# A mixture-of-experts block with one weight tile in an eleventh place, and its residual set up one expert later

## The chip, the cores and the metric

The kernel runs on one core of one Trainium2 chip. The metric is the device time of one execution in microseconds (us); the time quoted is the median over the runs of a kernel. Where a profile is read, it is one execution recorded by the hardware profiler, whose times count from the start of its span. TensorE is PE in the rows (PEld is its weight load), VectorE is DVE, ScalarE is ACT, GpSimd is POOL, and SyncE is SP; SP issues the transfers of the weights.

## What is computed

Two transformer blocks on 256 tokens of width 1024, all in fp32. The first is attention with 8 heads, a layer norm, a mixture of 32 experts with the best 4 for each token, and a layer norm. The second is a mixer of a gated linear recurrence and a short convolution, and a convolutional feed-forward network. The change lies in the mixture of experts, cut here to what matters:

```python
logits = xt @ w_router + b_router
top_logit, top_e = lax.top_k(logits, 4)
gate = softmax(top_logit)
# for each expert e, on the tokens that chose it:
h = xb @ w_gu[e] + b_gu[e]                    # [1024] -> [2048]
h_gate, h_up = split(h)
h_gate = minimum(h_gate, 7); h_up = clip(h_up, -7, 7)
act = h_gate * sigmoid(1.702 * h_gate) * (h_up + 1)
f = act @ w_down[e] + b_down[e]               # [1024] -> [1024]
# y = ALPHA * layer_norm(...) + sum over a token's experts of gate * f
```

Each expert has 8 MB of gate and up weights and 4 MB of down weights, so the 32 experts read 384 MB.

## The kernel before, in words

The experts go in order, 0 to 31, in batches of two, with 64 rows for each expert. For a batch the rows of its tokens are gathered by products with a one-hot matrix (`pgat`, L694) and the gates are put in place (`pw`, L763). For one expert `gate_up` (L777 to L800) multiplies four tiles of gate and up weights, c = 0 to 3, of 2 MB each, into the banks `pg` and `pu`. `swiglu` (L769 to L775) turns them into `at`, with four operations on VectorE and one on ScalarE. `transpose_act` transposes `at` by four products (`atp`, L805). `down_half` multiplies two tiles of down weights into `pd` (L818). Down products of expert e are issued one turn of the loop later, behind the gate and up products of expert e + 1, and with the last one of a batch the result is added into y, a tile named `xtok`.

y must hold its start value before that: `start_y` (L658 to L680) broadcasts the rows of the layer norm's gain and bias by eight small products into banks `lnr` (L259), scales and shifts the normed tokens on VectorE (L666 and L668, eight operations of 512 columns), transposes the gates (`gp`, L672), copies them (`GT`, L673), multiplies them with the down biases `bdn` (`pb`, L678, four products, eight instructions in the trace) and adds these to y (L679, four operations). In the kernel before it is called in the turn of expert 0.

The weights stream through ten places of 2 MB: six in a pool whose tiles are named `w` and four in one whose tiles are named `wb`. A list `loads` holds all transfers in order: first the attention's, then for each expert four gate and up tiles and the two down tiles of the expert before. In this text the 192 transfers of the experts are numbered from 1. `pump` (L183) issues the next ones on SP's queue, and `weight` asks it for nine tiles ahead of the one that is about to be multiplied. The n-th transfer takes the place of the (n - 10)-th, so SP waits until TensorE has multiplied that tile. SP's queue is in order: a transfer that waits holds all behind it.

Which instruction stands where on an engine is set by a scheduler that works on the program as it is written, except where `tc.no_sync_barrier()` parts it. On an engine the instructions then run in that order. In the middle, at expert 16, a branch handles experts with over 64 tokens (`overflow`); ahead of it SP waits until all transfers have landed (L847).

Of the kernel before, what the change touches and what calls it, by code (L numbers as in the profile page):

```python
# [10 lines left out]
F32 = mybir.dt.float32  # L11
# [11 lines left out]
P = 128  # L23
D = 1024
T = 256
NT = T // P
KT = D // P
NH = 8
NE = 32
TOPK = 4  # L30
FF = 1024
CAP = 64
NB = 2
SLOTS_A = 6
IN_B = (5, 7, 8, 9)
# [48 lines left out]
def block_kernel(ctx: ExitStack, tc: tile.TileContext, a: dict, out: bass.AP, dbg=None):  # L84
    nc = tc.nc
    dbg = dbg or {}
    mm = nc.tensor.matmul
    act = nc.scalar.activation
# [7 lines left out]
    pools = {}  # L96
# [25 lines left out]
    def load_run(t, w, r0, n):  # L122
# [2 lines left out]
        nc.sync.dma_start(t[:, 0:n * cols], w[r0:r0 + n * P, :]  # L125
                          .rearrange("(p k) c -> p (k c)", k=n))

    def load_run_last(t, w, r0, n):

        cols = w.shape[1]  # L130
        v = t[:, 0:n * cols].rearrange("p (k c) -> p k c", c=cols)
        for k, m in ((0, 2), (2, 1), (3, 1)):
            nc.sync.dma_start(v[:, k:k + m], w[r0:r0 + n * P, :]
                              .rearrange("(p k) c -> p k c", k=n)[:, k:k + m])
# [26 lines left out]
    for e in range(NE + 1):  # L161
        gu = [(("gu", e, c), load_run, (w_gu[e], c * 256, 2)) for c in range(4) if e < NE]
        dn = [(("dn", e - 1, c), load_run, (w_dn[e - 1], c * 512, 4)) for c in range(2) if e > 0]
        loads += dn + gu if e == OVF_AT else gu + dn
    end_moe = len(loads)
    loads[-1] = (loads[-1][0], load_run_last, loads[-1][2])
    W2_ORDER = (2, 1, 0, 3, 5, 6, 4)
# [16 lines left out]
    def pump(upto):  # L184
        while state["next"] < min(upto, len(loads)):
            i = state["next"]
            key, fn, args = loads[i]
            slot = (i - first_moe) % (SLOTS_A + len(IN_B))
            if first_moe <= i < end_moe and slot in IN_B:
                if "b" not in pools:  # L190
                    return
                t = pools["b"].tile([P, 4096], F32, name="wb", tag=f"w{IN_B.index(slot)}")
            else:
                t = wa.tile([P, 4096], F32, name="w", tag="w")
            fn(t, *args)
            tiles[key] = t
            state["next"] += 1

    def weight(key, ahead=SLOTS_A - 1):
        pump(order[key] + 1 + ahead)  # L200
        return tiles.pop(key)

    xtok = const.tile([P, NT, D], F32, name="xtok")
# [411 lines left out]
    with ExitStack() as c2:  # L615
# [4 lines left out]
        def xs_tile(n, shape):  # L620
            return p2.tile([P] + shape, F32, name=n, tag="xs")

        bdn = p2.tile([NE, D], F32, name="bdn", tag="ys")
        nc.gpsimd.dma_start(bdn, a["moe_b_down"][0])

        def gates():

# [125 lines left out]
        def weigh_batch(b):  # L753

            xs, oh = batches[b]
            wt = p2.tile([P, NT, NB, CAP], F32, name="wt", tag="wt")
            es = slice(b * NB, (b + 1) * NB)
            for tt in range(NT):
                V.tensor_tensor(wt[:, tt], oh[:, tt],
                                G[:, tt, es, None].to_broadcast([P, NB, CAP]), op=OP.mult)  # L760
            pw = bank("pw", [P, T], "t")
            for tt in range(NT):
                nc.tensor.transpose(pw[:, tt * P:(tt + 1) * P],  # L763
                                    wt[:, tt].rearrange("p e s -> p (e s)"), ident)
            wT = p2.tile([P, T], F32, name="wT", tag="wT", bufs=2)
            V.tensor_copy(wT, pw)
            batches[b] = [xs, wT]

        def swiglu(dst, pg, pu):  # L769
            gt = p2.tile([P, 512], F32, name="sw_g", tag="sw_g")  # L770
            V.tensor_scalar(gt, pg, LIMIT, None, op0=OP.min)  # L771
            act(dst, gt, AF.Sigmoid, scale=SW_ALPHA)  # L772
            V.tensor_mul(gt, gt, dst)
            V.tensor_scalar(dst, pu, LIMIT, -LIMIT, op0=OP.min, op1=OP.max)
            V.scalar_tensor_tensor(dst, dst, 1.0, gt, op0=OP.add, op1=OP.mult)  # L775

        def gate_up(e):  # L777
            xs, _ = batches[e // NB]
            col = (e % NB) * CAP
            pg = bank("pg", [P, 512], "g")  # L780
            pu = bank("pu", [P, 512], "u")
            sel_e = selb[:, e:e + 1].to_broadcast([96, CAP])
            for c in range(4):
                w = weight(("gu", e, c), AHEAD).rearrange("p (k c) -> p k c", c=2 * FF)
                for k in range(2):
                    kt = 2 * c + k
                    for q, dst in ((0, pg), (1, pu)):
                        for h in range(2):
                            c0 = q * FF + h * 512
                            mm(dst[h * CAP:(h + 1) * CAP, :], xs[:, kt, col:col + CAP],  # L790
                               w[:, k, c0:c0 + 512], start=(kt == 0), stop=(kt == KT - 1))
                if c == 0:
                    for q, dst in ((0, pg), (1, pu)):
                        for h in range(2):
                            c0 = q * FF + h * 512
                            mm(dst[h * CAP:(h + 1) * CAP, :], sel_e, bgu[:, c0:c0 + 512],
                               start=False, stop=False)
            at = p2.tile([P, 512], F32, name="at", tag="act")
            swiglu(at, pg, pu)
            return at  # L800

        def transpose_act(at, tag="aT", copy=nc.any.tensor_copy):
            pt = bank("atp", [P, 4, P], "t")
            for j in range(4):
                nc.tensor.transpose(pt[:, j, :], at[:, j::4], ident)  # L805
            aT = p2.tile([P, 4, P], F32, name="aT", tag=tag)
            copy(aT, pt)  # L807
            return aT

# [10 lines left out]

        def down_out(e, pd):
            if e % 2 == 0:
                ys_pair[e // 2] = p2.tile([P, 2, 512], F32, name="ys", tag="ys")
            ys = ys_pair[e // 2]
            o = (e % 2) * CAP
            for h in range(2):
                (nc.scalar.copy if h else V.tensor_copy)(  # L827
                    ys[o:o + CAP, h, :], pd[h][h * CAP:(h + 1) * CAP, :])
# [15 lines left out]
        def overflow():  # L844

            n = nc.values_load(cnti[0:1, 0:1], min_val=0, max_val=NE)
            with tc.If(n > 0), tc.For_i(0, n, 1) as e:  # L847
                for g in range(2):
# [30 lines left out]
                            mm(acc[q][h], sel_e, bgu[:, c0:c0 + 512], start=True, stop=False)  # L879
                    for kt in range(KT):  # L880
                        for q in range(2):
                            w = p2.tile([P, FF], F32, name="ow", tag="ys")
                            nc.sync.dma_start(
                                w, w_gu[bass.ds(e, 1), chan(kt), q * FF:(q + 1) * FF]
                                .rearrange("o p c -> p (o c)"))
                            for h in range(2):
                                mm(acc[q][h], xs[:, kt, :], w[:, h * 512:(h + 1) * 512],
                                   start=False, stop=(kt == KT - 1))
                    aT = []
                    for h in range(2):  # L890
                        at = p2.tile([P, 512], F32, name="oat", tag="act")
                        swiglu(at, acc[0][h], acc[1][h])
                        aT.append(transpose_act(at, ("aT", "sw_g")[h]))
                    pd = [bank(f"opd{h}", [P, 512], "tm"[h])
                          for h in range(2)]
                    for kt in range(KT):
                        w = p2.tile([P, D], F32, name="owd", tag="ys")
                        nc.sync.dma_start(w, w_dn[bass.ds(e, 1), kt // 4 * 512 + kt % 4:kt // 4 * 512 + 512:4, :]
                                          .rearrange("o p c -> p (o c)"))
                        for h in range(2):  # L900
                            mm(pd[h], aT[kt // 4][:, kt % 4, :], w[:, h * 512:(h + 1) * 512],
                               start=(kt == 0), stop=(kt == KT - 1))
# [56 lines left out]
        gates()  # L959
        forget_bounds()  # L960
        weigh_batch(0)
        for e in range(NE):
            if e == OVF_AT:
                finish(*prev)
                prev = None
                pump(order[("gu", e, 0)] + AHEAD + 1)
                overflow()
                tc.no_sync_barrier()
                make_batch(e // NB)
                weigh_batch(e // NB)  # L970
            if e == NE - 2:
                sums = open_sums()
            at = gate_up(e)
            if e == NE - 1:
                in_order.enter_context(tc.manual_schedule(engines={ET.PE, ET.DVE, ET.Activation}))
                mix_rows = finish_all(prev[1], at)
                break
            if e == 0:
                start_y()
            if e % NB == NB - 1 and e + 1 < NE and e + 1 != OVF_AT:  # L980
                make_batch(e // NB + 1)
                weigh_batch(e // NB + 1)
            if prev is not None:
                finish(*prev)
            prev = (e, transpose_act(at))
            if e == NE - 2:
                tail_rows()
# [485 lines left out]
```

## Time and profile before

| | us |
|---|---|
| median of three runs | 1391.38 |
| the runs | 1391.65, 1391.38, 1389.89 |
| the profiled execution | 1392.66 |
| its span in the trace | 1390.9 |
| TensorE busy | 1317.3 (95%) |
| VectorE busy | 518.6 (37%) |
| ScalarE busy | 326.2 (23%) |
| read from HBM | 476.17 MB, 343 GB/s over the span |

TensorE is busy for 95% of the span, but its matrix products are counted busy while they are queued as well, so this share alone does not say that it bounds the kernel. The mean rate of the transfers is 343 GB/s over the whole span; over the slices in which the experts run the page shows 424 to 428 GB/s in nearly all. The two shares are averages over stages with different limits, so a change in one stage is read from that stage's own rows.

### The profile page before, as it was taken

How to read it: one execution, taken by the hardware profiler on the slowest of the kernel's cores; microseconds unless marked ns; L12 is line 12 of the kernel's file. 1: busy time of each engine (PE TensorE's matmuls, PEld its weight loads, DVE VectorE, ACT ScalarE, POOL GpSimd, SP SyncE). 2: the span in 40 equal slices, each digit the busy share in tenths (PEclk: the TensorE clock that was granted, in tenths of full speed). 3: DMA queues.
4: the chain of work that ended last, by engine and by line, in shares of the span. 5: the costliest groups of instructions: out<-in, count | busy, mean ns of one | idle time of the engine just before them, and what ended most of it. 6: DMA issues, size and time to landing. Idle time of an engine off the chain costs nothing.

```text
span 1390.9 us, 16965 instructions
## 1 busy us (share of the span) xinstructions
PE 1317.3 (95%) x7162; PEld 748.0 (54%) x7162; DVE 518.6 (37%) x923; ACT 326.2 (23%) x574; POOL 54.2 (4%) x52
## 2 busy tenths in 40 slices
PE   9999999999999998799989989898999999999998
PEld 8887344334334332343433324233336998899997
DVE  4665322222222112221221212211115686777776
ACT  4553010011011000011000001000114444655554
POOL 2100000000000000000000000000003321000000
PEclk9999999999999999999999999999999999999999
DMA  8967999999999999989999999999999424555500
GB/s 257 373 273 292 377 427 426 426 427 427 427 427 425 428 428 424 426 352 428 427 427 426 428 427 427 426 426 426 429 423 388 184 89 155 187 200 190 181 1 31
DMA packets 75381, 478.78 MB, mean 344 GB/s; under 512 B 4972, under 2 KB 32180, under 8 KB 50724
## 3 DMA queue, kind: packets, MB, share of 16 engines
q1 hardware_dynamic: 74804, 477.09, 84.2%
q8 instruction: 58, 0.95, 0.3%
q0 software_dynamic: 496, 0.56, 0.1%
q14 instruction: 23, 0.19, 0.0%
HBM read 476.17 MB, written 1.06 MB: 343 GB/s over the span
## 4 chain that ended last, share of the span: by engine, by line
PE 31%; DMA 24%; DVE 2%; ACT 1%; issue 0%; POOL 0%; DVEq 0%; ACTq 0%; SPq 0%; POOLq 0%
DMA wb<-in_moe_w_gate_up_dram 10%; PE pu L266 9%; DMA w<-in_moe_w_gate_up_dram 6%; DMA w<-in_moe_w_down_dram 6%; PE pq L266 4%; DMA wb<-in_moe_w_down_dram 3%; PE pg L790 3%; PE pu L790 2%; PE pd L818 2%; PE fa L270 1%; PE fa L272 1%; PE fa L271 1%; PE px L1240 1%; PE pgat L694 1%; PE mo L271 1%; PE mo L272 1%
## 5 line engine op out<-in xcount | busy, mean ns | idle before, releaser
L790 PE MATMUL pg<-w,xs 128*64 128x512 f32 x616 | 181.5, 600 | 11.0 <-DMA w<-in_moe_w_gate_up_dram 11.0
L790 PE MATMUL pu<-w,xs 128*64 128x512 f32 x616 | 181.5, 593 | 0.0
L771 DVE TENSOR_SCALAR sw_g<-pg 128x512 f32<-128x512 f32 x32 | 22.1, 692 | 402.6 <-PE pg L790 402.6
L818 PE MATMUL pd<-w,aT 128*64 128x512 f32 x624 | 144.2, 601 | 14.6 <-DMA w<-in_moe_w_down_dram 14.0
L772 ACT ACTIVATE at<-sw_g 128x512 f32<-128x512 f32 x32 | 20.1, 630 | 549.8 <-DVE sw_g L771 549.8
L790 PE MATMUL pg<-wb,xs 128*64 128x512 f32 x408 | 114.7, 599 | 9.4 <-DMA wb<-in_moe_w_gate_up_dram 9.4
L790 PE MATMUL pu<-wb,xs 128*64 128x512 f32 x408 | 114.3, 596 | 0.0
L818 PEld LDWEIGHTS pd<-w,aT 128*64 128x64 f32 x624 | 45.0, 138 | 101.8 <-issue 78.4
L790 PEld LDWEIGHTS pu<-w,xs 128*64 128x64 f32 x616 | 52.3, 137 | 87.4 <-issue 87.1
L1009 ACT CAST hi<-w 128x1024 fp32r<-128x1024 f32 x75 | 78.4, 1048 | 87.0 <-PE pu L266 40.1
L790 PEld LDWEIGHTS pg<-w,xs 128*64 128x64 f32 x616 | 48.0, 137 | 93.4 <-issue 83.5
L818 PE MATMUL pd<-wb,aT 128*64 128x512 f32 x400 | 91.7, 597 | 4.8 <-DMA wb<-in_moe_w_down_dram 4.8
L827 DVE COPY ys<-pd 64x512 f32<-64x512 f32 x32 | 21.9, 683 | 187.3 <-PE pd L818 187.3
L1010 DVE TENSOR_TENSOR lo<-w,hi 128x1024 fp32r<-128x1024 f32 x60 | 74.1, 1234 | 43.7 <-ACT hi L1009 41.1
L694 PEld LDWEIGHTS pgat<-oh,h 128*128 128x128 f32 x512 | 66.5, 207 | 23.5 <-issue 21.9
L694 PE MATMUL pgat<-oh,h 128*128 128x128 f32 x512 | 71.8, 298 | 6.8 <-DVE oh L688 6.2
L1010 POOL TENSOR_TENSOR lo<-w,hi 128x1024 fp32r<-128x1024 f32 x15 | 36.0, 2404 | 1001.6 <-DVE st L1107 934.4
L807 ACT COPY aT<-atp 128x512 f32<-128x512 f32 x32 | 18.7, 585 | 227.1 <-PE pd L818 186.8
L790 PEld LDWEIGHTS pu<-wb,xs 128*64 128x64 f32 x408 | 32.6, 137 | 57.7 <-issue 56.9
L790 PEld LDWEIGHTS pg<-wb,xs 128*64 128x64 f32 x408 | 30.1, 136 | 60.3 <-issue 53.0
L818 PEld LDWEIGHTS pd<-wb,aT 128*64 128x64 f32 x400 | 27.6, 137 | 56.3 <-issue 47.8
L841 PE MATMUL pc<-ys,wT 128*128 128x512 f32 x112 | 53.3, 608 | 1.6 <-DVE ys L827 1.6
(321 smaller groups left out, 1841.4 us busy)
## 6 DMA issues: line engine op xcount, KB each, us to landing
w<-in_moe_w_gate_up_dram SPq DMA_DIRECT2D x77, 2048.0 KB
wb<-in_moe_w_gate_up_dram SPq DMA_DIRECT2D x51, 2048.0 KB
w<-in_moe_w_down_dram SPq DMA_DIRECT2D x38, 2048.0 KB
wb<-in_moe_w_down_dram SPq DMA_DIRECT2D x25, 2048.0 KB
w<-in_ffn_w_up_dram SPq DMA_DIRECT2D x22, 1024.0 KB
w<-in_w_in_dram SPq DMA_DIRECT2D x6, 2048.0 KB
w<-in_a_w_in_dram SPq DMA_DIRECT2D x5, 2048.0 KB
w<-in_ffn_w_down_dram SPq DMA_DIRECT2D x5, 2048.0 KB
```

What stands on the lines that cost most here:

```text
L266: mm(psum_ap, lhs[:, kt, :], rhs[:, kt, :], start=(i == 0 and kt == kts[0]), stop=(i == len(pairs) - 1 and kt == kts[-1]))
L271: mm(psum_ap, lh, rl, start=False, stop=False)
L272: mm(psum_ap, ll, rh, start=False, stop=last)
L694: mm(pg[:, j, :], h1[:, tt, chan(kt)], batches[b][1][:, tt].rearrange("p e s -> p (e s)"), start=start, stop=stop)
L771: V.tensor_scalar(gt, pg, LIMIT, None, op0=OP.min)
L772: act(dst, gt, AF.Sigmoid, scale=SW_ALPHA)
L790: mm(dst[h * CAP:(h + 1) * CAP, :], xs[:, kt, col:col + CAP], w[:, k, c0:c0 + 512], start=(kt == 0), stop=(kt == KT - 1))
L818: mm(pd[h][h * CAP:(h + 1) * CAP, :], lhs, w[:, k, h * 512:(h + 1) * 512], start=(c == 0 and k == 0), stop=(c == 1 and k == 3))
L827: (nc.scalar.copy if h else V.tensor_copy)(ys[o:o + CAP, h, :], pd[h][h * CAP:(h + 1) * CAP, :])
L841: mm(pc, lhs[:, tt * P:(tt + 1) * P], ys[:, h, :], start=True, stop=True)
L1009: nc.scalar.copy(hi, piece)
L1010: (nc.gpsimd if on_pool else V).tensor_sub(lo, piece, f32(hi))
```

## The change

One tile gets a place of its own. The last of expert 0's four gate and up tiles (c = 3) is taken out of the fourth position of the list and put in the eleventh (`ONCE`). It is loaded as two transfers of 1 MB, one into `xtok`, which holds nothing yet, and one into a new tile `late`. `late` then also takes the parts of three tiles that are gone: the buffer `sw_g` and the result `at` of `swiglu`, and the down product's copy `ys`. All other tiles go through the ten places as before, so the places shift by one expert tile from there on.

Since `xtok` holds weights until expert 0's gate and up products are done, y can't be set up ahead of them: `start_y` is called in the turn of expert 1, and the down biases are loaded into `late` behind expert 0's products. Expert 0's `gate_up` is called ahead of the loop, with a barrier of the order behind it.

```diff
+    def load_run_rows(t, w, r0, n):
+        for k in range(n):
+            nc.sync.dma_start(t[k], w[r0:r0 + n * P, :]
+                              .rearrange("(p k) c -> p k c", k=n)[:, k])
...
+    ONCE = first_moe + SLOTS_A + len(IN_B)
+    key, _, args = loads.pop(first_moe + 3)
+    loads.insert(ONCE, (key, load_run_rows, args))
...
-            slot = (i - first_moe) % (SLOTS_A + len(IN_B))
-            if first_moe <= i < end_moe and slot in IN_B:
+            slot = (i - first_moe - (i > ONCE)) % (SLOTS_A + len(IN_B))
+            if i == ONCE:
+                if "once" not in pools:
+                    return
+                t = pools["once"]
+            elif first_moe <= i < end_moe and slot in IN_B:
...
-        pump(order[key] + 1 + ahead)
+        upto = order[key] + 1 + ahead
+        if order[key] != ONCE:
+            pump(upto + (order[key] < ONCE < upto))
...
-        bdn = p2.tile([NE, D], F32, name="bdn", tag="ys")
-        nc.gpsimd.dma_start(bdn, a["moe_b_down"][0])
+        late = p2.tile([P, 2 * FF], F32, name="late")
+        late_sw, late_act = (late[:, i * 512:(i + 1) * 512] for i in range(2))
+        late_ys = late[:, FF:2 * FF]
+        pools["once"] = [xtok.rearrange("p n d -> p (n d)"), late]
+        pump(ONCE + 1)
+        bdn = late_ys[0:NE]
...
-            gt = p2.tile([P, 512], F32, name="sw_g", tag="sw_g")
+            gt = late_sw
...
-            at = p2.tile([P, 512], F32, name="at", tag="act")
+            at = late_act
...
-                ys_pair[e // 2] = p2.tile([P, 2, 512], F32, name="ys", tag="ys")
+                ys_pair[e // 2] = late_ys.rearrange("p (h c) -> p h c", c=512)
...
         weigh_batch(0)
+        at = gate_up(0)
+        tc.no_sync_barrier()
         for e in range(NE):
...
-            at = gate_up(e)
+            if e > 0:
+                at = gate_up(e)
...
             if e == 0:
+                nc.gpsimd.dma_start(bdn, a["moe_b_down"][0])
+            if e == 1:
                 start_y()
```

On TensorE, where expert 0's products end and those of expert 1 begin, there stood before (`lnr` and `gp` belong to `start_y`, `cmain` holds the identity matrix of a transpose):

```order
L259 MATMUL lnr_1466<-rows,selb 128x256
L672 MATMUL gp<-cmain,G 32x128 x2
L790 MATMUL pg<-w,xs 64x512 x2
L790 MATMUL pu<-w,xs 64x512
L259 LDWEIGHTS selb
L259 MATMUL lnr_1471<-rows,selb 128x256
```

Now there stands at that place (`xtok` and `late` are the two halves of the tile in the eleventh place):

```order
L813 MATMUL pg<-xtok,xs 64x512 x2
L813 MATMUL pu<-xtok,xs 64x512 x2
L813 MATMUL pg<-late,xs 64x512 x2
L813 MATMUL pu<-late,xs 64x512 x2
L828 MATMUL atp<-cmain,late 128x128 x4
L813 MATMUL pg<-w,xs 64x512 x2
L813 MATMUL pu<-w,xs 64x512 x2
```

The products of `start_y` stood between the two experts and inside the second's; now the transposes of expert 0's activation follow its products directly, and expert 1's products stand behind these transposes.

Further on, in the products of expert 1 and behind them on the same engine, there stood before:

```order
L805 MATMUL atp<-cmain,at 128x128 x4
L790 MATMUL pg<-wb,xs 64x512
L790 MATMUL pu<-wb,xs 64x512 x2
L790 MATMUL pg<-wb,xs 64x512
L678 MATMUL pb<-bdn,GT 128x512 x4
```

```order
L790 MATMUL pg<-wb,xs 64x512 x2
L790 MATMUL pu<-wb,xs 64x512 x2
L694 MATMUL pgat<-oh,h_67 128x128 x16
L763 MATMUL pw<-cmain,wt 128x128 x2
L818 MATMUL pd<-wb,aT 64x512 x16
```

Now there stands behind expert 1's last products:

```order
L275 LDWEIGHTS selb
L275 MATMUL lnr_1533<-rows,selb 128x256
L699 MATMUL pb<-late,GT 128x512 x4
L715 MATMUL pgat<-oh,h_67 128x128 x16
L784 MATMUL pw<-cmain,wt 128x128 x2
L844 MATMUL pd<-wb,aT 64x512 x16
L828 MATMUL atp<-cmain,late 128x128 x4
```

All products of `start_y` moved out of those of expert 1 to behind them, ahead of the gather of the next batch (`pgat`) and of expert 0's down products (`pd`).

On VectorE, at the end of `start_y`, there stood before:

```order
L668 TENSOR_TENSOR xtok<-xtok,lnr_1471 128x512
L775 SCALAR_TENSOR_TENSOR at<-at,sw_g 128x512
L668 TENSOR_TENSOR xtok<-xtok,lnr_1471 128x512
L668 TENSOR_TENSOR xtok<-xtok,lnr_1476 128x512 x2
L673 COPY GT<-gp 32x256
L679 SCALAR_TENSOR_TENSOR xtok<-xtok,pb 128x512 x4
```

Now there stands:

```order
L796 SCALAR_TENSOR_TENSOR late<-late 128x512
L687 TENSOR_TENSOR xtok<-h_67,lnr_1523 128x512
L689 TENSOR_TENSOR xtok<-xtok,lnr_1528 128x512 x2
L689 TENSOR_TENSOR xtok<-xtok,lnr_1533 128x512 x2
L694 COPY GT<-gp 32x256
L700 SCALAR_TENSOR_TENSOR xtok<-xtok,pb 128x512 x4
```

The copy `GT`, for which the products `pb` wait, stands as before behind all eight operations on y; these were woven into expert 0's `swiglu` and are now woven into expert 1's.

## Rows read from the trace of the kernel before

**Rows 1.** Chain that ended last, middle of the run: start us, us, what.

```profile
633.97 39.36 DMA wb<-in_moe_w_gate_up_dram
...
949.71 3.68 PE pd L818 x16
```

**Rows 2.** Stretches: length; busy PE, PEld, DVE, ACT, POOL; granted clock, DMA share, GB/s.

```profile
130.00:135.00 5.00, 5.00 (x32) 4.30 (x32) 3.85 (x23) 1.13 (x4) 0.00 (x0) 0.78 0.60 256
135.00:140.00 5.00, 5.00 (x25) 1.84 (x24) 0.97 (x6) 1.66 (x3) 0.00 (x0) 1.00 0.09 21
165.00:170.00 5.00, 5.00 (x24) 1.64 (x22) 0.00 (x0) 0.00 (x0) 0.00 (x0) 0.87 0.66 213
330.00:400.00 70.00, 69.26 (x330) 26.08 (x328) 16.93 (x34) 8.39 (x17) 0.00 (x0) 1.00 1.01 426
400.00:1050.00 650.00, 594.35 (x2754) 230.03 (x2752) 126.23 (x234) 58.37 (x112) 0.00 (x0) 0.99 1.00 422
```

**Rows 3.** Timeline of SP, transfers 11, 15, 16 and 19: start us, us, what.

```profile
138.99 0.33 SPq L125 DMA_DIRECT2D w<-in_moe_w_gate_up_dram  x1
...
155.87 0.33 SPq L125 DMA_DIRECT2D w<-in_moe_w_down_dram  x1
...
165.98 0.33 SPq L125 DMA_DIRECT2D wb<-in_moe_w_down_dram  x1
...
180.86 0.33 SPq L125 DMA_DIRECT2D wb<-in_moe_w_gate_up_dram  x1
```

**Rows 4.** Timeline, experts 0 and 1, PE and DVE: start us, us, what.

```profile
148.87 0.69 DVE L771 TENSOR_SCALAR sw_g<-pg 128x512 f32<-128x512 f32 x1 [12.17 <-PE pg L790]
149.62 0.61 PE L259 MATMUL lnr<-rows,selb 96*128 96x256 bf16 x4
156.64 0.40 DVE L673 COPY GT<-gp 32x256 f32<-32x256 f32 x1
158.75 3.88 PE L678 MATMUL pb<-bdn,GT 32*128 32x512 f32 x8
172.98 4.04 PE L694 MATMUL pgat<-oh,h 128*128 128x128 f32 x32
177.16 7.09 PE L818 MATMUL pd<-wb,aT 128*64 128x512 f32 x32
```

**Rows 5.** Timeline of later experts, where nothing of `start_y` stands.

```profile
184.86 1.08 PE L790 MATMUL pg<-w,xs 128*64 128x512 f32 x4
...
188.78 1.03 PE L790 MATMUL pg<-w,xs 128*64 128x512 f32 x4
...
199.08 3.60 PE L818 MATMUL pd<-w,aT 128*64 128x512 f32 x16
...
304.73 0.69 DVE L771 TENSOR_SCALAR sw_g<-pg 128x512 f32<-128x512 f32 x1 [12.63 <-PE pg L790]
...
308.91 0.75 PE L805 MATMUL atp<-cmain,at 128*128 128x128 f32 x4
309.58 3.65 PE L818 MATMUL pd<-wb,aT 128*64 128x512 f32 x16
```

**Rows 6.** Stretches with a lower granted clock; columns as in rows 2.

```profile
162.00:164.00 2.00, 2.00 (x6) 0.44 (x6) 1.58 (x4) 0.00 (x0) 0.00 (x0) 0.72 1.00 426
164.00:166.00 2.00, 2.00 (x8) 0.73 (x6) 0.00 (x0) 0.00 (x0) 0.00 (x0) 0.50 0.58 238
580.00:585.00 5.00, 1.36 (x6) 1.39 (x7) 1.30 (x6) 0.00 (x0) 0.00 (x0) 0.77 1.00 413
585.00:590.00 5.00, 5.00 (x27) 5.00 (x26) 1.37 (x4) 0.00 (x0) 0.00 (x0) 0.54 1.00 418
```

**Rows 7.** Timeline at the gather behind the overflow branch's start, PE.

```profile
583.64 6.65 PE L694 MATMUL pgat<-oh,h 128*128 128x128 f32 x32 [6.20 <-DVE oh L688]
```

**Rows 8.** SP at the overflow branch: its waits by line, and its next issue.

```profile
L847 SPq EVENT_SEMAPHORE  x8: 17/17/17, 593.6 to 619.7; - x8
...
620.17 0.35 SPq L125 DMA_DIRECT2D w<-in_moe_w_gate_up_dram  x1
```

More of the change, by code (lines that the diff above doesn't have):

```diff
@@ L783, in gate_up @@
             for c in range(4):
-                w = weight(("gu", e, c), AHEAD).rearrange("p (k c) -> p k c", c=2 * FF)
+                w = weight(("gu", e, c), AHEAD)
+                if (e, c) != (0, 3):
+                    w = [w[:, k * 2 * FF:(k + 1) * 2 * FF] for k in range(2)]
                 for k in range(2):
@@ L790, in gate_up @@
                             mm(dst[h * CAP:(h + 1) * CAP, :], xs[:, kt, col:col + CAP],
-                               w[:, k, c0:c0 + 512], start=(kt == 0), stop=(kt == KT - 1))
+                               w[k][:, c0:c0 + 512], start=(kt == 0), stop=(kt == KT - 1))
                 if c == 0:
@@ L805, in transpose_act @@
                 nc.tensor.transpose(pt[:, j, :], at[:, j::4], ident)
-            aT = p2.tile([P, 4, P], F32, name="aT", tag=tag)
+            if tag == "sw_g":
+                aT = late_sw.rearrange("p (j s) -> p j s", s=P)
+            else:
+                aT = p2.tile([P, 4, P], F32, name="aT", tag=tag)
             copy(aT, pt)
@@ L881, in overflow @@
                         for q in range(2):
-                            w = p2.tile([P, FF], F32, name="ow", tag="ys")
+                            w = late_ys
                             nc.sync.dma_start(
@@ L890, in overflow @@
                     for h in range(2):
-                        at = p2.tile([P, 512], F32, name="oat", tag="act")
+                        at = late_act
                         swiglu(at, acc[0][h], acc[1][h])
@@ L896, in overflow @@
                     for kt in range(KT):
-                        w = p2.tile([P, D], F32, name="owd", tag="ys")
+                        w = late_ys
                         nc.sync.dma_start(w, w_dn[bass.ds(e, 1), kt // 4 * 512 + kt % 4:kt // 4 * 512 + 512:4, :]
```

## The prediction

> **What bounds the kernel now.** I read three views: the chain that ended last, the stretches of the experts, and SP's issues. In the middle of the run the chain is one transfer of weights behind the other, piece after piece of some 39 us, until TensorE takes over at 949.71 and leads to the end [rows 1]. The stretches agree: the DMA share is 1.01 from 330 to 400 and 1.00 from 400 to 1050, at 426 and 422 GB/s [rows 2]. So what bounds this part is the stream of weights, and a stretch in which it stands still is not made up later: what it loses early arrives at the end in full. A transfer is 2.097 MB, at 427 GB/s (the page's rate in full slices) 4.91 us.
>
> It stands still in two places near the first experts: the share is 0.60 in 130:135 and 0.09 in 135:140, 2.0 + 4.5 = 6.5 us lost, and 0.66 in 165:170, 1.7 us lost [rows 2]. SP's issues say why. Ten transfers fill the ten places; the 11th is issued only at 138.99, when expert 0's first tile is multiplied. Later the 15th, 16th and 19th go at 155.87, 165.98 and 180.86 [rows 3]. The 16th came late (the second hole). From it on there is no reserve: three transfers of 4.91 us behind 165.98 make 180.7, and the 19th is issued at 180.86, just as the stream would run dry. The 19th takes the place of expert 0's first down tile. Its issue in the changed kernel therefore says how far the whole stream moves.
>
> **The change, part by part.** The eleventh place lets one transfer more go ahead of 138.99: 4.91 us of the first hole are filled. The price is two issues in place of one, about 0.33 us of SP [rows 3], at a time when ten transfers are still queued; nothing. The first ten have landed at about 130 + 0.60 x 5 = 133 [rows 2], so the eleventh tile lands at about 138; its products are the last quarter of expert 0's, which end at 149.6, 14.22 / 4 = 3.6 us before [rows 4, 5]. TensorE doesn't wait for it.
>
> From there the n-th transfer (n from 15 on) waits for the same tile as before. So I follow TensorE to expert 0's down products.
>
> 1. Expert 0's products end as before, and the bank `pg` is handed to VectorE at 148.87 [rows 4]. The transposes of the activation now follow at once, so TensorE must wait for the whole of `swiglu`, which before lay beside expert 1's products. Undisturbed it takes 308.91 - 304.73 = 4.18 us from its first operation to the transposes, and these 0.67 to the next product [rows 5]. Expert 1's products then start at 148.87 + 4.18 + 0.67 = 153.72.
> 2. Undisturbed gate and up products take 199.08 - 184.86 = 14.22 us [rows 5]: they end at 167.94. In the kernel before they ended at 172.98, since `start_y` and a lower clock lay in them [rows 4, 6]. So far 5.0 us are gained.
> 3. Now `start_y` begins, with nothing of TensorE beside it. From its first broadcast to the end of the `GT` copy it took 156.64 + 0.40 - 149.62 = 7.42 us, VectorE working through eight operations on y and three of `swiglu` [rows 4]; the same eleven stand there now. So 175.4. The `pb` products take 3.88 [rows 4]: 179.2.
> 4. Gather and gates take 177.16 - 172.98 = 4.18 [rows 4]: expert 0's down products start at 183.4. In the kernel before the 19th was issued 180.86 - 177.16 = 3.70 behind their start [rows 3, 4]; now at 187.1.
>
> That is 6.3 us later than 180.86, at full clock. Does the stream run dry until then? The 12th now goes at 138.99, and three transfers behind it make 153.7; the 15th waits for expert 1's first tile, 188.78 - 184.86 = 3.92 behind the start of the products [rows 5], until 157.6. Four transfers from there make 177.3, and 187.1 is 9.8 later. So the filled hole is given back as a wait of the 15th (3.9 us) and of the 19th (9.8 us), and all that lies earlier in the stream, its two smaller transfers too, is covered by the latter.
>
> **The clock.** A lower clock would come on top. Two places of before show it. Right behind the `pb` products it was 0.72 and then 0.50 in 162:166, that is 1.2 GHz for a part of it [rows 6]; this cost 0.28 x 2 + 0.50 x 2 = 1.6 us. Where TensorE had waited 6.20 us for VectorE it was 0.77 and 0.54 in 580:590 [rows 6], 1.15 + 2.3 = 3.5 us, and the gather took 6.65 in place of 4.04 [rows 4, 7]. In the changed kernel TensorE idles for most of the 7.42 us ahead of `pb`, save for broadcasts of some 0.6 us a group [rows 4]: like the second place, and I take its 3.5. The bounds are 0 (the low clock may fall into the wait itself) and 3.88 + 2.6 = 6.5 (both `pb` at half speed and the gather as in [rows 7]). For the wait of 3.4 us for `swiglu`, at 149.6 to 153.05, no row of before is alike; between 0 and the 1.6 of the first place I take 0.7.
>
> The Trainium skill has a rule that speaks against this term: by "TensorE: Matmul & The Clock Gate", section "Loop structure matters more than you think", a copy of the result out of PSUM by the vector engine "doesn't break PE warmth". By it the clock would cost nothing and the sum would stay at 6.3. The trace of before differs at one place: VectorE takes `pb` out of PSUM there, and the granted clock behind it is 0.50 [rows 6].
>
> **Other edits.** `late` holds in one tile what three tiles held; were a write to it to wait for the last reader of any part, `swiglu` of expert 0 would wait for the last products, 149.62 - 148.87 = 0.8 us more [rows 4]; I take 0. Later experts have had their readers by then. The down biases, 128 KB or 0.3 us at the stream's rate, have from 150 to 175 to come by the pool's queue. The barrier of the order adds no wait by itself. Behind the 19th both the stream and TensorE are late by the same amount, so the order of the rest, the overflow branch and the end stay as they were.
>
> Sum: 6.3 + 3.5 + 0.7 = 10.5 us. The profiled execution was 1392.66, 1.28 above the median; the difference is added to the median: 1391.38 + 10.5 = 1401.9.
>
> **Rivals.**
>
> - Slower, without the clock: 1391.38 + 6.3 = 1397.7. For it: the low clock may fall into the wait, where it costs nothing. Against it: [rows 6], both places.
> - Faster, because only the first hole counts. The mechanism is the eleventh place: the stream is one transfer further at 139, and if the place of the 19th came free by then, 4.91 us stay gained: 1386.5; with the second hole gone as well, 1.7 more, 1384.8. It decides at the 19th: it must be issued by 180.86 - 4.91 = 175.9 in place of 187.1. For it speaks that expert 1's products end 5 us earlier; against it that `pb`, gather and 3.70 us of down products, 11.8 us of work on the same engine, stand between, besides the 7.4 on VectorE. It would need `start_y` to lie beside products, which the order excludes.
> - No change, 1391.4: the loss vanishes at the overflow branch. SP waits there for all transfers, the last of them at 619.7, and issues the next at 620.17 [rows 8]. If TensorE's work set that time, and not the stream, a late stream would be caught up. Against it: the stream's share is 1.00 up to there, and the wait ends with a transfer's landing, which moves with the stream.
>
> "DMA: Bandwidth & Descriptors" of the Trainium skill, section "Rules for kernel authors", advises to issue a transfer early, compute, and wait late. By this rule alone the change would bring the 4.91 us of the faster rival. The trace shows its limit here: the issue of the 19th is set by a product's end and not by when SP could have issued it [rows 3, 4].
>
> **How the numbers follow.** Slower in one of the two forms 0.85 (with the clock's loss 0.62, without 0.23), no change 0.07, faster 0.08. The predicted time is that of the first, 1401.9. All bounds together reach from 6.3 to 6.3 + 6.5 + 1.6 + 0.8 = 15.2, 1397.7 to 1406.6. The range takes these in and goes down by another 1.7, since the 4.18 of `swiglu` and the 7.42 of `start_y` could come shorter than in these rows: 1396.0 to 1406.6; it leaves out the two rivals on the other side, 0.15. Within 0.2% (2.8 us) is what a measurement of this kernel can't tell from no change.
>
> **What would show it.** In the profile of the changed kernel: the DMA share near 1 up to 138, one dip around 156 to 159 and a hole of some 10 us or more up to the issue of the 19th at 187 to 193; TensorE idle for 3.4 us ahead of the transposes at 153 and for 7 us ahead of `pb`; a granted clock near 0.5 at `pb` or the gather; then a stream at 1.00, and the same length from there to the end. The prediction is wrong if the 19th is issued ahead of 181, if `pb` starts within 2 us of the last products of expert 1, or if the overflow branch starts no later than before although the 19th was late.

## The result, and the profile after

The changed kernel takes 1403.16 us (median of four runs, 1402.2 to 1404.35) against 1391.52 of the kernel before (four runs, 1389.89 to 1394.01). The ratio is 1.0083, with a 95% interval of 1.0071 to 1.0096: 11.6 us slower. The forecast was 1401.9, slower.

The first view is SP's timeline of the changed kernel (start us, us, what). It answers to [rows 3]; the eleventh place is the two rows of L131.

```profile
119.49 0.39 SPq L131 DMA_DIRECT2D xtok<-in_moe_w_gate_up_dram  x1
119.93 0.43 SPq L131 DMA_DIRECT2D late<-in_moe_w_gate_up_dram  x1
138.21 7.63 SPq L125 DMA_DIRECT2D w<-in_moe_w_gate_up_dram  x3
159.09 4.20 SPq L125 DMA_DIRECT2D w<-in_moe_w_down_dram  x2
...
169.83 0.33 SPq L125 DMA_DIRECT2D w<-in_moe_w_gate_up_dram  x1
194.19 3.76 SPq L125 DMA_DIRECT2D wb<-in_moe_w_gate_up_dram  x2
```

The row at 159.09 begins with the 15th transfer, that at 194.19 with the 19th: 13.3 us behind the 180.86 of before. Between the 18th at 169.83 and the 19th, SP issues nothing for 24 us. What that does to the stream is in the stretches of the same execution, columns as in [rows 2]:

```profile
135.00:140.00 5.00, 5.00 (x26) 2.02 (x27) 0.42 (x1) 1.28 (x1) 0.00 (x0) 1.00 0.56 175
140.00:145.00 5.00, 5.00 (x26) 1.67 (x24) 0.00 (x0) 0.00 (x0) 0.00 (x0) 1.00 0.88 374
...
155.00:160.00 5.00, 5.00 (x20) 1.54 (x18) 0.00 (x0) 0.00 (x0) 0.00 (x0) 0.69 0.11 40
...
180.00:185.00 5.00, 5.00 (x9) 1.89 (x8) 1.94 (x4) 0.00 (x0) 0.00 (x0) 0.50 0.06 23
185.00:190.00 5.00, 5.00 (x30) 5.00 (x30) 1.90 (x7) 0.00 (x0) 0.00 (x0) 0.62 0.00 0
190.00:195.00 5.00, 5.00 (x27) 1.95 (x28) 1.23 (x5) 1.50 (x4) 0.00 (x0) 1.00 0.00 0
...
330.00:400.00 70.00, 69.26 (x340) 28.11 (x341) 14.27 (x28) 5.11 (x10) 0.00 (x0) 1.00 1.01 426
400.00:1050.00 650.00, 597.30 (x2774) 230.79 (x2772) 130.14 (x242) 61.17 (x118) 0.00 (x0) 0.99 1.00 424
```

The first hole, 6.5 us in [rows 2], is down to 0.44 x 5 + 0.12 x 5 = 2.8. In its place stand 0.89 x 5 = 4.5 us ahead of the 15th transfer and 4.7 + 5.0 + 5.0 = 14.7 ahead of the 19th. From 330 on the stream is full again, as before.

The reason is on TensorE, in its timeline without the products of experts 0 and 1; it answers to [rows 4]:

```profile
151.75 1.13 PE L828 MATMUL atp<-cmain,late 128*128 128x128 f32 x4 [2.84 <-DVE late L796]
...
169.72 0.61 PE L275 MATMUL lnr<-rows,selb 96*128 96x256 bf16 x4
...
177.25 7.16 PE L699 MATMUL pb<-late,GT 32*128 32x512 f32 x8 [2.36 <-issue]
184.33 6.01 PE L715 MATMUL pgat<-oh,h 128*128 128x128 f32 x32
...
190.49 7.09 PE L844 MATMUL pd<-wb,aT 128*64 128x512 f32 x32
```

The transposes wait for `swiglu`; the broadcasts begin only behind expert 1's products, and 7.4 us later come the bias products, which take 7.16 us in place of 3.88, and the gather, 6.01 in place of 4.04. Expert 0's down products start at 190.49, and 3.70 us later the 19th transfer goes, as in the kernel before (177.16 and 180.86). The clock of these stretches:

```profile
152.00:154.00 2.00, 2.00 (x8) 1.00 (x9) 0.50 (x3) 0.59 (x1) 0.00 (x0) 0.50 0.88 328
154.00:156.00 2.00, 2.00 (x6) 0.47 (x4) 0.00 (x0) 0.00 (x0) 0.00 (x0) 0.50 0.87 274
156.00:158.00 2.00, 2.00 (x8) 0.49 (x6) 0.00 (x0) 0.00 (x0) 0.00 (x0) 0.50 0.00 0
...
178.00:180.00 2.00, 2.00 (x4) 0.66 (x2) 0.68 (x1) 0.00 (x0) 0.00 (x0) 0.50 1.07 459
...
182.00:184.00 2.00, 2.00 (x3) 0.38 (x2) 0.69 (x1) 0.00 (x0) 0.00 (x0) 0.50 0.00 0
...
186.00:188.00 2.00, 2.00 (x11) 2.00 (x11) 0.00 (x0) 0.00 (x0) 0.00 (x0) 0.50 0.00 0
```

It is 0.50 (1.2 GHz) behind both waits, although the engine is counted busy for all of each stretch.

The 13.3 us don't all arrive. At the overflow branch the rows that answer to [rows 8] are now:

```profile
L873 SPq EVENT_SEMAPHORE  x8: 17/17/17, 562.8 to 592.2; - x8
...
592.29 1.49 SPq L125 DMA_DIRECT2D wb<-in_moe_w_gate_up_dram  x3
```

SP's last wait is at 592.2 and the next transfer goes at 592.29, 28 us earlier than before: SP reaches the branch with 98 transfers issued in place of 106. (It is 98 in the traces of all kernels of this document that have the barrier, and 106 in all that don't.) The stretches around the hole there, before and after:

```profile
610.00:615.00 5.00, 5.00 (x27) 1.98 (x25) 0.00 (x0) 0.00 (x0) 0.00 (x0) 1.00 0.95 400
615.00:620.00 5.00, 5.00 (x25) 1.78 (x22) 0.15 (x1) 0.00 (x0) 0.00 (x0) 1.00 0.26 108
620.00:625.00 5.00, 5.00 (x38) 4.22 (x38) 4.00 (x9) 0.63 (x1) 0.00 (x0) 1.00 0.79 259
```

```profile
585.00:590.00 5.00, 4.21 (x13) 1.37 (x10) 2.22 (x4) 0.58 (x1) 0.00 (x0) 1.00 0.86 364
590.00:595.00 5.00, 1.00 (x5) 0.38 (x4) 2.00 (x6) 0.00 (x0) 0.00 (x0) 1.00 0.48 129
```

That is 0.25 + 3.7 + 1.05 = 5.0 us lost before and 0.7 + 2.6 = 3.3 after: 1.7 come back. The last experts start their sum (`sum`, an operation that both kernels have once per half) at

```profile
1051.73 0.70 PE L913 MATMUL sum<-ys,wT 128*128 128x512 f32 x1
```

```profile
1054.19 7.07 PE pd L844 x31
...
1062.02 0.70 PE L939 MATMUL sum<-late,wT 128*128 128x512 f32 x1 [0.65 <-DVE late L853]
```

before and after, 10.3 later. (The row at 1054.19 is from the chain that ended last, after.) So 13.3 - 1.7 = 11.6 are carried to the last experts, and 1.3 go there: in the kernel before, the chain ran over TensorE from 949.71 [rows 1], so the stream's end had some slack; after, it runs over transfers until 1054.19. The span grew by 10.7. All these figures are of one profiled execution of each kernel.

### The profile page after: what moved, and what is told of

Its sections match the earlier page's. It is cut to its first block, busy times and chain, and to the rows that moved or that the text cites. A ratio compares the mean times of both kernels' runs of the same rounds, so it can differ in the third digit from the quotient of the medians.

```text
span 1401.6 us, 16955 instructions
## 1 busy us (share of the span) xinstructions
PE 1321.5 (94%) x7162; PEld 752.7 (54%) x7162; DVE 518.6 (37%) x923; ACT 326.6 (23%) x574; POOL 53.5 (4%) x52
## 4 chain that ended last, share of the span: by engine, by line
DMA 33%; PE 22%; DVE 2%; ACT 0%; issue 0%; DVEq 0%; SPq 0%; ACTq 0%
DMA wb<-in_moe_w_gate_up_dram 11%; PE pu L282 9%; DMA wb<-in_moe_w_down_dram 8%; DMA w<-in_moe_w_gate_up_dram 7%; DMA w<-in_moe_w_down_dram 6%; PE pq L282 4%; PE fa L286 1%; PE fa L288 1%; PE fa L287 1%; PE px L1271 1%; PE mo L286 1%; PE mo L288 1%; PE mo L287 1%; PE pd L844 1%; PE pv L1131 0%; PE warm L293 0%
## 5 line engine op out<-in xcount | busy, mean ns | idle before, releaser
L813 PE MATMUL pg<-w,xs 128*64 128x512 f32 x608 | 183.1, 607 | 13.8 <-DMA w<-in_moe_w_gate_up_dram 13.3
L792 DVE TENSOR_SCALAR late<-pg 128x512 f32<-128x512 f32 x32 | 22.1, 692 | 428.4 <-PE pg L813 428.4
L844 PE MATMUL pd<-w,aT 128*64 128x512 f32 x608 | 137.7, 596 | 11.9 <-DMA w<-in_moe_w_down_dram 7.7
L793 ACT ACTIVATE late<-late 128x512 f32<-128x512 f32 x32 | 20.2, 630 | 541.1 <-DVE late L792 541.1
L844 PE MATMUL pd<-wb,aT 128*64 128x512 f32 x384 | 87.2, 596 | 6.7 <-DMA wb<-in_moe_w_down_dram 6.7
L853 DVE COPY late<-pd 64x512 f32<-64x512 f32 x32 | 21.9, 684 | 187.2 <-PE pd L844 187.2
L867 PE MATMUL pc<-late,wT 128*128 128x512 f32 x112 | 53.5, 610 | 1.6 <-DVE late L853 1.6
```

Source lines behind the costliest of these rows:

```text
L844: mm(pd[h][h * CAP:(h + 1) * CAP, :], lhs, w[:, k, h * 512:(h + 1) * 512], start=(c == 0 and k == 0), stop=(c == 1 and k == 3))
L853: (nc.scalar.copy if h else V.tensor_copy)(ys[o:o + CAP, h, :], pd[h][h * CAP:(h + 1) * CAP, :])
L867: mm(pc, lhs[:, tt * P:(tt + 1) * P], ys[:, h, :], start=True, stop=True)
```

## The experiments

The theory: the time follows the issue of the 19th transfer, which waits for expert 0's down products; late are `swiglu`'s wait, the set-up of y and the clock behind the two waits. The rivals: the eleventh place costs something of its own, or gains by itself; the barrier makes the loss; the clock is a side effect.

**Y in the first turn again.** The changed kernel with

```diff
             if e == 0:
                 nc.gpsimd.dma_start(bdn, a["moe_b_down"][0])
-            if e == 1:
                 start_y()
```

> The changed kernel with the set-up of y back in the turn of expert 0; the eleventh place, the first products ahead of the loop and the barrier stay. My theory: the time follows the issue of the 19th transfer, so of expert 0's down products. The broadcasts fill part of the wait for swiglu, and no wait of 7 us stands behind expert 1's products; the 19th is issued at 182 to 186, and the time is 1391 to 1396 us. Rival, that the eleventh place is worth its 4.9 us as soon as y is out of the way: 1386 to 1387 us. Rival, that the wait for swiglu at the barrier makes the loss: 1400 us or more.

Measured: 1395.51 us (ten runs), ratio to before 1.0036 (1.0017 to 1.0055). The runs fell into two groups: seven at 1393.8 to 1396.4 with a mean granted clock of 0.991 to 0.996, and three at 1403.4 to 1404.7 with 0.985 to 0.989. The profiled execution is of the upper group (1404.67). Its stretches:

```profile
152.00:154.00 2.00, 0.37 (x3) 0.41 (x3) 1.90 (x5) 0.00 (x0) 0.00 (x0) 1.00 0.96 410
...
156.00:158.00 2.00, 2.00 (x4) 0.29 (x2) 2.00 (x5) 0.58 (x1) 0.00 (x0) 0.50 0.59 201
...
160.00:165.00 5.00, 5.00 (x8) 1.46 (x8) 1.36 (x3) 0.00 (x0) 0.00 (x0) 0.50 0.00 0
165.00:170.00 5.00, 5.00 (x10) 1.21 (x6) 0.83 (x2) 0.00 (x0) 0.00 (x0) 0.50 0.00 0
170.00:175.00 5.00, 5.00 (x15) 1.89 (x16) 1.09 (x3) 0.00 (x0) 0.00 (x0) 0.51 0.20 39
```

Behind TensorE's wait for `swiglu` the clock is 0.50 until 175, through the bias products and the first products of expert 1, and the stream stands still from 158 to about 174. The times of the lower group are where I expected them, and the 4.9 us of the eleventh place don't show in them; no execution of that group was profiled, so the issue of its 19th is not on record. The upper group I had not expected.

**No barrier.** The changed kernel with expert 0's products back in the loop:

```diff
-        at = gate_up(0)
-        tc.no_sync_barrier()
         for e in range(NE):
...
-            if e > 0:
-                at = gate_up(e)
+            at = gate_up(e)
```

> The changed kernel with expert 0's products in the loop and no barrier behind them; y is set up in the second turn. The order then puts expert 1's products ahead of expert 0's last tile, and there is no wait for swiglu between the two experts. My theory: the chain of y, the gather and the down products still lie behind each other; the 19th is issued at about 187, 7 us late, and the time is 1398 us (1396 to 1401). What the barrier did at the overflow branch (some 2 us gained there) is gone. Rival, that the barrier and its wait make the loss: 1391 us or less.

Measured: 1399.24 us, ratio 1.0064 (1.0047 to 1.008). The 19th transfer:

```profile
186.78 3.76 SPq L125 DMA_DIRECT2D wb<-in_moe_w_gate_up_dram  x2
```

At 187, as expected. The loss without the barrier is 7.6 us, against 11.6 with it: the larger part of it doesn't come from the barrier. What the other 4.0 are is answered by the run with the barrier alone, below.

**Only y in the second turn.** The kernel before with one line:

```diff
-            if e == 0:
+            if e == 1:
                 start_y()
```

> The kernel before with one edit, the set-up of y in the turn of expert 1. My theory: expert 1's products end at about 164.5, then come 7.4 us of set-up, the products with the down biases at a lower clock (7 us), the gather (4 to 6 us) and 3.7 us of down products: the 19th is issued at 187.5 to 189.5 in place of 180.9, and the time is 1399 us (1397 to 1401). Rival, that the loss comes from the eleventh place, its two transfers or the shared tile: 1391 to 1392 us.

Measured: 1401.42 us, ratio 1.0073 (1.0056 to 1.009). TensorE and SP:

```profile
172.47 7.16 PE L678 MATMUL pb<-bdn,GT 32*128 32x512 f32 x8 [2.37 <-issue]
179.56 6.31 PE L694 MATMUL pgat<-oh,h 128*128 128x128 f32 x32
```

```profile
189.71 0.33 SPq L125 DMA_DIRECT2D wb<-in_moe_w_gate_up_dram  x1
```

This one line costs 9.8 us, the larger part of the loss, with no eleventh place, no shared tile and no barrier; bias products and gather run at the lower clock here too. The issue and the time lie slightly above the ranges expected.

**Only the barrier.** The kernel before with expert 0's products ahead of the loop:

```diff
         weigh_batch(0)
+        at = gate_up(0)
+        tc.no_sync_barrier()
         for e in range(NE):
...
-            at = gate_up(e)
+            if e > 0:
+                at = gate_up(e)
```

> The kernel before with one edit, expert 0's gate and up products ahead of the loop with the barrier behind them. My theory: TensorE waits for swiglu before expert 1's products, partly beside the broadcasts of y; the 19th is issued 3 to 6 us late, some 2 us come back at the overflow branch, whose drain on SP's queue starts 8 transfers earlier: 1392 to 1396 us. The difference to the run with the eleventh place and y in the first turn says what the eleventh place is worth: nothing by my theory, 4.9 us by the rival.

Measured: 1395.32 us (eight runs), ratio 1.0042 (1.0019 to 1.0066); six runs at 1393.9 to 1395.5 and two at 1404.1 and 1404.7. So the barrier alone, with the order that it brings, costs 3.7 us, about as much as the changed kernel loses beyond the run without it (4.0): it is a part of the loss, the smaller one. Against the run with the eleventh place and y in the first turn (1395.51) there is no difference, and the medians of the two lower groups are 0.8 us apart (1394.33 there, 1395.12 here): behind that order the eleventh place is worth nothing that can be told from noise. The profiled execution is of the lower group here, 1395.32:

```profile
156.00:158.00 2.00, 2.00 (x7) 0.42 (x6) 1.95 (x4) 0.00 (x0) 0.00 (x0) 0.50 0.97 418
158.00:160.00 2.00, 2.00 (x6) 0.66 (x4) 0.47 (x1) 0.00 (x0) 0.00 (x0) 0.95 0.87 369
160.00:165.00 5.00, 5.00 (x20) 1.65 (x21) 2.68 (x6) 0.00 (x0) 0.00 (x0) 1.00 0.02 7
```

The clock is back at 158, and the stream stands still for 5 us in place of 16. The two profiles, of kernels with the same order on TensorE here, show what parts the groups; that the other runs of each group look like these is argued from their mean clocks and not shown.

**The waits filled.** The changed kernel with small products nobody reads in both waits (the first of them shown):

```diff
+            if e == 0:
+                warm(bank("warm", [P, 512], "t"), 26)
             prev = (e, transpose_act(at))
```

> The changed kernel with small products into a spare bank, whose result nobody reads, put into TensorE's two waits: 26 ahead of the transposes of expert 0's activation, 56 between the broadcasts and the products with the down biases. My theory: the low clock took 3.4 us behind the first wait and about 5 us at the bias products and the gather; with the waits filled the clock stays up, the 19th transfer is issued at 185 to 187 in place of 194.2, and the time is 1395 us (1393.5 to 1397). Rival, that the waits themselves and not the clock make the loss: 1402 to 1404 us.

Measured: 1398.87 us, ratio 1.0047 (1.003 to 1.0064). The timeline:

```profile
151.30 3.05 PE L293 MATMUL warm<-idle 128*1 128x256 bf16 x26
154.29 0.73 PE L832 MATMUL atp<-cmain,late 128*128 128x128 f32 x4
...
177.37 3.88 PE L703 MATMUL pb<-late,GT 32*128 32x512 f32 x8
181.18 4.04 PE L719 MATMUL pgat<-oh,h 128*128 128x128 f32 x32
```

```profile
178.00:180.00 2.00, 2.00 (x6) 0.57 (x4) 1.30 (x2) 0.00 (x0) 0.00 (x0) 1.00 0.94 401
```

```profile
189.06 0.33 SPq L125 DMA_DIRECT2D wb<-in_moe_w_gate_up_dram  x1
```

The granted clock is 1.00 in all stretches from 148 to 188. Bias products and gather take 3.88 and 4.04 us again, as in [rows 4]: the clock had made 3.3 + 2.0 us of them. `swiglu` of expert 0 started at 150.54 in this execution and at 148.09 in that of the changed kernel; from there to the 19th it is 38.5 us against 46.1, 7.6 less. The time fell by only 4.3 and lies above the range expected, as does the 19th's issue: 2.5 us of the difference between 7.6 and the gain is that later start, which lies ahead of the edit. (Starts differ so from execution to execution: the first transfer behind the full ring is issued between 136.8 and 140.7 in the profiled ones.) The small products also cost something: `GT` was ready at 176.29 + 0.41 = 176.70 and the bias products began at 177.37, 0.7 us later, where it was 0.1 in the changed kernel. Without that the gain at the 19th would be nearer 8.1 than 7.6.

**The gather behind the down products.** The kernel before with the second batch's `make_batch` and `weigh_batch` behind `finish` in the turn of expert 1:

```diff
-            if e % NB == NB - 1 and e + 1 < NE and e + 1 != OVF_AT:
+            if e % NB == NB - 1 and e + 1 < NE and e + 1 != OVF_AT and e > 1:
                 make_batch(e // NB + 1)
...
             if prev is not None:
                 finish(*prev)
+            if e == 1:
+                make_batch(1)
+                weigh_batch(1)
```

> The kernel before with one edit: the gather of the second batch and its gates behind expert 0's down products in place of ahead of them. The place of the 19th transfer comes free 4.2 us earlier, at about 176.7. My theory: the stream gets to the 19th only at 180.7, since the 16th went at 166.0, so nothing is gained: 1391.5 us (1390.5 to 1392.5). Rival, that expert 0's down products alone set the stream, whatever lies ahead: 4.2 us less, 1387 us.

Measured: 1390.74 us (ten runs), ratio 0.9995 (0.9986 to 1.0005): nothing. The 19th did go earlier, by 5.0 us (it is the first of these two):

```profile
175.89 3.76 SPq L125 DMA_DIRECT2D wb<-in_moe_w_gate_up_dram  x2
```

So a place that is free earlier brings nothing while the stream is not there yet; both sides of the 19th count, the place and the queue ahead.

**The order by hand, with and without the eleventh place.** Expert 1's products directly behind expert 0's, with the pieces of `start_y` between its tiles, and the gather behind the down products. `y_rows`, `y_gates` and `y_bias` are the parts of `start_y`; `between` holds what is called behind each of the four tiles.

```diff
+        with tc.manual_schedule(engines={ET.PE}):
+            at0 = gate_up(0, (lambda: weigh_batch(0),))
+            nc.gpsimd.dma_start(bdn, a["moe_b_down"][0])
+            y_rows((0, 1))
...
+            at = gate_up(1, (one, two, lambda: y_bias(hold["GT"], (0,)),
+                             lambda: y_bias(hold["GT"], (1,))))
+            finish(0, hold["aT"])
+            make_batch(1)
+            weigh_batch(1)
+            prev = (1, transpose_act(at))
+        for e in range(2, NE):
```

> The eleventh place kept, and TensorE's order for experts 0 and 1 written out by hand: expert 1's products directly behind expert 0's, with the broadcasts of y, the transposes of expert 0's activation and the bias products between its tiles, then expert 0's down products, then the gather. There is no barrier. My theory: the 15th transfer is issued at about 154.5, the 19th at 173 to 175, and of the holes of before (10.0 us) 2.5 stay at 138 to 140 and 1.5 ahead of the 15th: 6 us less than before, 1385.5 us (1384 to 1387.5). Rival, that the eleventh place costs something of its own: 1391 us or more.

> The same order written out by hand, but without the eleventh place (the ten places and tiles of the kernel before). My theory: the hole at 133 to 140 stays, those at 165 and ahead of the 19th go: 2.5 us less than before, 1389 us (1388 to 1390.5). The difference to the run with the eleventh place, 3.5 us, is what that place is worth once the order lets it count. Rival, that the order alone brings the gain: the same time in both.

Measured: 1384.0 us with the eleventh place, ratio 0.9941 (0.9924 to 0.9957), and 1388.57 without it, ratio 0.9972 (0.996 to 0.9983). With it, on TensorE and SP:

```profile
161.04 1.98 PE L704 MATMUL pb<-late,GT 32*128 32x512 f32 x4
166.54 1.98 PE L704 MATMUL pb<-late,GT 32*128 32x512 f32 x4
168.45 7.09 PE L851 MATMUL pd<-wb,aT 128*64 128x512 f32 x32
```

```profile
172.14 3.76 SPq L125 DMA_DIRECT2D wb<-in_moe_w_gate_up_dram  x2
```

The down products start 22 us earlier than in the changed kernel, and the bias products run at the full clock between products of expert 1. The same eleventh place that was worth nothing behind the other order is worth 4.6 us here by the two medians. How much exactly stays open between some 2 and 5 us: the profiled executions are 3.4 apart (1388.71 and 1385.33), and the repeat of the first kernel below is only 2.2 further under its kernel before than the second is under its own.

**The filled wait, y in the first turn.** The first experiment's kernel with 47 small products between and behind the broadcasts of `start_y` (as an edit of the changed kernel):

```diff
+            wb_ = bank("warm", [P, 512], "u")
...
                 bcast_row(row, (R_LNG, R_LNB)[k // 2][0], k % 2)
+                warm(wb_, (0, 28, 11, 8)[k])
...
-            if e == 1:
                 start_y()
```

> The run with y in the first turn (eleventh place, barrier), whose ten times fell into two groups, seven at 1394 to 1396 and three at 1403 to 1405 us, with 47 small products without a reader put into TensorE's wait for swiglu and the broadcasts. My theory: the upper group is the clock, which after that wait stayed at 1.2 GHz for 20 us in the profiled execution; with the wait filled it stays up, and there is one group: 1392.5 us (1391 to 1394.5), no time above 1398. Rival, that the two groups come from something else, the transfers for instance: again a quarter of the times or more at 1402 or above.

Measured: 1398.7 us (four runs: 1395.16, 1397.72, 1399.69, 1400.47), ratio 1.0055 (1.004 to 1.0071). A miss: no run above 1402, but the median is 6 us above what I expected. So neither the theory nor the rival is confirmed, and what makes the two groups stays open. The edit also moved the transposes of the activation behind all broadcasts. In the profiled execution (1395.16) the clock didn't fall near this place; the three others were not profiled, and why they are 3 to 5 us longer stays open.

**The order by hand again, and with a barrier.** The second has one line more:

```diff
+        tc.no_sync_barrier()
         with tc.manual_schedule(engines={ET.PE}):
```

> The eleventh place with the order written by hand, run again beside the next one on the same chip: 1384 us (1383 to 1385.5).

> The same with one edit, a barrier of the order ahead of expert 0's products. TensorE's order stays; on SP's queue the load of the overflow's count moves from behind the 106th transfer to behind the 11th, and the branch from behind the 106th to behind the 98th. My theory: that, and nothing on TensorE, gave back 1 to 2 us at the overflow branch in all kernels with a barrier; the hole there is that much shorter: 1382.7 us (1381.8 to 1383.6). Rival, that the gain there only made up for a stream that was late: 1384 us as without it.

Measured on one chip: 1386.17 us, ratio 0.9964 (0.995 to 0.9977), and 1385.53, ratio 0.9956 (0.9942 to 0.997). Both lie above the ranges expected, the first by 0.7 and the second by 1.9 us. They can't be told apart, so that the barrier's place on SP's queue gains something by itself at the overflow branch is not shown. The order by hand with the eleventh place is faster than the kernel before on the same chip in both of its measurements, by 8.0 and 5.6 us.

## Why the prediction was right

The direction, the mechanism and the time came as forecast; the terms did not all, and that the time lies within 1.3 us of the forecast is luck as far as two errors cancelled (3 and 4 below).

1. *The place that decides.* The 19th transfer's issue set the shift of the stream. One line that moves y shows it (19th at 189.71, 1401.42 us), and the gather behind the down products shows its other half. In the profiled executions in which the 19th was late, the time follows it (both against the kernel before, 180.86 and 1392.66):

   | kernel | 19th later, us | time longer, us |
   |---|---|---|
   | filled wait, y in the first turn | 2.7 | 2.5 |
   | only the barrier | 2.8 | 2.7 |
   | no barrier | 5.9 | 5.1 |
   | the waits filled | 8.2 | 6.9 |
   | only y in the second turn | 8.9 | 8.6 |
   | y in the first turn | 12.0 | 12.0 |
   | the changed kernel | 13.3 | 10.7 |

2. *The sum at full clock, 6.3 us.* With the waits filled the 19th went 38.5 us behind the start of expert 0's `swiglu`; in the kernel before it was 180.86 - 148.87 = 32.0 [rows 3, 4]. The difference is 6.5, of which the small products themselves made some 0.6 (they held the bias products back). In the changed kernel the wait for `swiglu` came shorter (151.75 - 148.09 = 3.7 in place of 4.18) and the set-up of y as in the rows (176.74 + 0.41 - 169.72 = 7.43 against 7.42).
3. *The clock, 3.5 + 0.7 = 4.2 us.* This term was mis-sized: by the comparison in the run with filled waits it is 7.6, or some 8.1 without what the small products held back. I had taken the bias products and the gather together at the price of [rows 6]; they lost 3.3 and 2.0, near the upper bound that I had named (3.9 and 2.6 at most). And I had put the wait for `swiglu` at 0.7, while behind it the clock was 0.50 from 152 to 158: 3 us lost at half speed, which is also above the 1.6 that I had named as that term's bound.
4. *What hid it.* "The order of the rest, the overflow branch and the end stay as they were" failed. The branch on SP's queue moved ahead of eight transfers and its hole lost 1.7 us less, and the last experts took in 1.3. Of the 13.3 us at the 19th, 10.7 arrived in the span, and this made up for most of the clock term; the range held the time for a reason that the prediction didn't have. That the branch's place gave the 1.7 back is read off the stretches and not shown by an experiment: the run with y in the first turn has the same early branch, and its execution is longer by as much as its 19th was late. The sentence that called an overflow branch no later than before a sign against it was wrong as well: it was earlier, although the 19th was late.
5. *The rivals.* That the eleventh place is worth its 4.9 us was right as a mechanism and wrong in this order: nothing behind the barrier's order, some 2 to 5 behind the order by hand. That the barrier costs some 4 us of its own stood in no rival; the sum has it only as the wait for `swiglu` and the clock behind that wait.

Of the Trainium skill's rule in "TensorE: Matmul & The Clock Gate", section "Loop structure matters more than you think", that a copy out of PSUM doesn't break PE warmth, the runs show limits. In its example the next products follow at once. So they do in the order by hand, and there it holds: the bias products between expert 1's tiles take 1.98 us for four instructions, at the pace of the run with filled waits (3.88 for eight), and the granted clock is 1.00 from 140 to 200. In the changed kernel TensorE waits for VectorE ahead of them, and they take 7.16; so the rule did not speak against the clock term, as the prediction had it. And in the kernel before the products follow at once too, and still the clock behind the bias products is 0.50 in 164:166 [rows 6]; why is not shown.

## What to carry to other kernels

Where a stream of transfers bounds a kernel, look for the one transfer that is issued without reserve, and follow the engine that frees its place: work put ahead of that point can delay the whole stream (here by 13.3 us), while taking work away from there brings nothing as long as the stream has not come so far; and a place added to the ring was worth nothing or 2 to 5 us, by the order alone. A chain through another engine that lay beside products is dear when it stands alone: its time, and what the products behind it lose to the clock. And a barrier in the order can move instructions on a queue far from where it stands, so look at that queue to the end.

## What the runs showed that I had not expected

TensorE's clock stayed at 1.2 GHz long after a wait, with the engine counted busy throughout from 156 on: from about 155 to 175 us in one execution of the kernel with y in the first turn, while in one of the kernel with the barrier alone, with the same order there, it was back at 158. Ten runs of the one and eight of the other fell into two groups some 9 us apart. A median over few runs of such a kernel can land in either. That the clock makes the groups fits these two profiles, but the run that was to show it missed.
